# A two-block transformer forward pass: the query rotation later, the forget-gate sums in three pieces, one wide product per norm

## The chip, the cores and the metric

The kernel runs on one core of a Trainium2 chip. The metric is the device time of one execution in microseconds (us), the median of several runs. In the texts PE is TensorE, DVE is VectorE, ACT is ScalarE, POOL is GpSimd and SP is SyncE, which issues most of the transfers.

## The reference, cut to what matters

One sequence of 512 tokens and width 1024, all in float32, goes through two blocks. What the change touches is the root-mean-square norm ahead of each projection, the forget gate of the first attention and the rotation of the latent attention's queries:

```python
def rms_norm(x, g):
    y = x * lax.rsqrt(jnp.mean(x * x, axis=-1, keepdims=True) + NORM_EPS)
    return y * g

# first block, mixer
proj = xn @ w_in
qa, ka, va, fa, cq, ckv, kr, ga, gb = jnp.split(proj, splits, axis=-1)
log_f = jax.nn.log_sigmoid(fa + b_forget)
ya = forgetting_attention(qa, ka, va, log_f)      # uses c = cumsum(log_f) over the tokens
qb = rms_norm(cq, q_a_norm_g) @ w_q_up            # q_nope and q_rope of 8 heads
q_rope = apply_rope(q_rope, cos, sin)
kv = rms_norm(ckv, kv_a_norm_g) @ w_kv_up         # k_nope and v of 8 heads
yb = latent_attention(q_nope, q_rope, k_nope, rope(kr), v)
h = h + (gate_a * (ya @ w_branch_a) + gate_b * (yb @ w_branch_b)) @ w_out
h = h + swiglu(rms_norm(h, norm_ffn_g))
# second block: x + 0.5 swiglu(norm), a second mixer, x + 0.5 swiglu(norm), a last norm
```

## The kernel before, in words

The activations lie transposed, features on the 128 partitions and the 512 tokens on the free axis, as eight tiles of 128x512. To keep float32 accuracy at the speed of the reduced float32 type (F32R), every operand is split into a high and a low F32R part (ACT makes the high, DVE or POOL the low), and each product is three products (`mm3`): high by high, high by low, low by high. Weights stream from memory on SP's queue and are split by ACT (L235) and DVE (L236).

A planner places the instructions: the program is traced in order, and each engine's queue gets its instructions by that order, a later one being let ahead where the planner's own estimate says that an earlier one isn't ready. What is in a queue runs strictly in order. `weave` traces two generators in turn: the attention of 16 heads as the main one, and as filling the remaining projections (`pair`, `gates`, `prepare_b`).

The norm chain has four links. While the eight tiles of a hidden state come out of a projection, `sq_add` squares each on ACT (L449) and adds it to an accumulator on POOL (L451). `sum_rows` (L417) adds over the partitions with four one-column products against ones, in plain float32; the trace records each plain float32 product as two products. `rstd` makes the reciprocal root (L422 on DVE, the power on POOL, L411). `spread` turns the 128x4 result into a 128x512 tile with the same value on every partition: the values are split in two (L433 and L370), each part is multiplied into a diagonal (L437, tile `diag`), and two F32R products with ones (L440) add up the columns; ACT copies the sum out (L442). `spread` is called eight times: in `first_mixer`, twice in `prepare_b` (for the two latent norms), once in the first feed-forward stage, twice in the second, once in `second_mixer` and once in the last feed-forward stage. In the feed-forward stages it is a hook between two groups of 24 products.

`forget_rows` (called after the first of three latent groups, L828) makes the log forget gates, their running sums over the tokens with products against a triangle and ones (L1041, L1042), and turns them by transposes (L1057) into the tile `crow` (L1059). For each head a POOL transfer (L1089) brings two rows of `crow` into the keys' second tile, which the scores (L1095, L1096) read.

`prepare_b` makes the latent attention's inputs: both spreads, the query features (L852 evacuates on DVE), the rotated part `qr` (ACT, L867), `rope_q` (L868: four POOL and eight DVE operations, all of line L1003), the key features (L852 again), v (ACT, L876) and `rope_kr`, whose transposes are recorded at L692.

Of the kernel before, what the change touches and what calls it, by code (L numbers as in the profile page):

```python
# [333 lines left out]
class Build:  # L334
# [78 lines left out]
    def sum_rows(self, acc):  # L413

        b = self.bank("s")[:, 0:NT]
        for tt in range(NT):
            self.nc.tensor.matmul(b[:, tt:tt + 1], lhsT=acc[:, tt * P:(tt + 1) * P], rhs=self.ones[:, 0:1], start=True, stop=True)  # L417
        return b
# [8 lines left out]
    def spread(self, r, tag, pool=None):  # L427

        nc = self.nc
        b = self.bank("s")  # L430
        rh = self.small.tile([P, NT], F32R, tag="rh", name=self.nm("rh"), bufs=1)
        rl = self.small.tile([P, NT], F32, tag="rl", name=self.nm("rl"), bufs=1)
        nc.vector.tensor_copy(rh, r)  # L433
        self.lo(rl, r, rh)
        dg = self.small.tile([P, 2, 512], F32R, tag="diag", name=self.nm("diag"), bufs=1)
        for n, x in enumerate((rh.bitcast(F32), rl)):
            nc.vector.tensor_tensor(  # L437
                out=dg[:, n, :].rearrange("p (a b) -> p a b", a=NT), in0=self.ident[:, None, :].to_broadcast([P, NT, P]),
                in1=x[:, :, None].to_broadcast([P, NT, P]), op=ALU.mult)
            nc.tensor.matmul(b, lhsT=self.ones_r, rhs=dg[:, n, :], start=n == 0, stop=n == 1)  # L440
        o = (pool or self.small).tile([P, 512], F32, tag=tag, name=self.nm(tag), bufs=1)
        nc.scalar.copy(o, b)  # L442
        return o

    def sq_add(self, acc, x, first, scale=None, tmp=None, eng=None):

        nc = self.nc
        dst = acc if first else tmp if tmp is not None else self.small.tile([P, 512], F32, tag="sq", name=self.nm("sq"), bufs=1)
        nc.scalar.activation(dst, x, AF.Square, scale=1.0 if scale is None else scale)  # L449
        if not first:  # L450
            (eng or nc.gpsimd).tensor_tensor(out=acc, in0=acc, in1=dst, op=ALU.add)  # L451
# [269 lines left out]
    def load_start(self, yp):  # L721
# [42 lines left out]
        V.memset(self.halfpi, float(np.pi / 2))  # L764
        self.ones_r = one(P, "ones_r", F32R)
        return acc, xt
# [8 lines left out]
    def first_mixer(self, acc0, xt, ey, yp):  # L775
# [5 lines left out]
        for c in range(2):  # L781
            def ev(tt, b, c=c):
                if tt == 0 and c == 0:
                    self.r_tok = self.rstd(self.sum_rows(acc0), D)
                nc.scalar.activation(tokA[:, tt, c * 276:(c + 1) * 276], b, AF.Copy, scale=self.r_tok[:, tt:tt + 1])

            for _ in self.tokens(f"t1{c}", (2, 2, 2, 2) if c else self.FIRST, 276, self.xh, self.xl, self.TOKTAGS[c], ev):
                n += 1
                if n % 4 == 0 and self.squares:
                    self.squares.pop(0)()  # L790
            if c == 0:
                nc.gpsimd.tensor_copy(self.ones_r, self.ones)
                self.rb = self.spread(self.r_tok, "rb")
# [24 lines left out]
        for m in range(3):  # L818
# [8 lines left out]
            if m == 0:  # L827
                self.forget_rows(tokA, yp)  # L828

# [7 lines left out]
        def prepare_b():  # L837
# [21 lines left out]
            for t in range(2):  # L859
# [6 lines left out]
                for i in range(2):  # L866
                    nc.scalar.activation(qr[:, 2 * t + i, :], b[:, i * 256:(i + 1) * 256], AF.Copy, scale=rq[:, 2 * t + i:2 * t + i + 1])  # L867
            self.rope_q(qr)  # L868
            w = self.ws.next("kv")
            self.ws.run_ahead()  # L870
            yield from feats(1, w, ch[2:], cl[2:], rbkv)
            for tt in range(NT):
                b = self.bank("mm")
                sl = slice(tt * P, (tt + 1) * P)
                self.mm3(b, ch[2][:, sl], cl[2][:, sl], w[0][:, 0, 512:1024], w[1][:, 0, 512:1024], True, True)
                nc.scalar.activation(v[:, tt, :], b, AF.Copy, scale=rkv[:, tt:tt + 1])  # L876
                yield 640.0
            self.rope_kr(kr, yp)
            B["ready"] = True
# [147 lines left out]
    def forget_rows(self, tokA, yp):  # L1027
# [10 lines left out]
        V.tensor_scalar(out=f, in0=f, scalar1=0.0, scalar2=None, op0=ALU.min)  # L1038
        V.tensor_tensor(out=f, in0=f, in1=l, op=ALU.subtract)
        b = self.bank("s")  # L1040
        nc.tensor.matmul(b[:, 0:32], lhsT=self.cst[:, C_TRI:C_TRI + P], rhs=f, start=True, stop=True)  # L1041
# [10 lines left out]
        self.hi(cs[:, :, :, 0], c4, scale=-8.0)  # L1052
        self.lo(cs[:, :, :, 1], c4, cs[:, :, :, 0], scale=-8.0)
        b = self.bank("s")
        cs2 = cs.rearrange("p t h c -> p t (h c)").bitcast(F32)
# [104 lines left out]
    def out_product(self, key, mh, ml, src, gain, accs):  # L1160
# [5 lines left out]
        for m in range(KD):  # L1166
# [5 lines left out]
            self.put_x(m, xs[m], self.gain(gain, m))  # L1172
            self.sq_add(accs, xs[m], m == 0)

# [707 lines left out]
    def main(self):  # L1882
# [30 lines left out]
        def out0(m, x):  # L1913
            self.put_x(m, x, self.gg[:, m:m + 1])
            self.sq_add(acc1, x, m == 0)
            self.sq_add(acc2, x, m == 0, scale=gf(m))

        self.ffn("f0", 1.0, lambda m: self.gain("norm_ffn_g", m), [sums, spread], out0)
# [23 lines left out]
        def out1(m, x):  # L1942
            self.put_x(m, x, self.gain("mix_norm_2", m))
            self.sq_add(acc3, x, m == 0)
            nc.sync.dma_start(out=self.spill["x2"][m], in_=x)
# [120 lines left out]
```

## Time and profile before

| | us |
|---|---|
| median of 3 runs | 2049.75 |
| lowest and highest | 2049.63, 2051.26 |
| the profiled execution's own time | 2051.97 |
| its span, first to last instruction | 2050.2 |
| TensorE busy in the span | 2016.3 (98%) |
| VectorE, ScalarE, GpSimd busy | 1467.2, 1040.4, 549.4 |

The page gives busy time by engine first. The view of waits lists, for an engine, what ended its idle times. A timeline row has the start, the duration, the engine, the line, the operation with its output and inputs, the shape, the count and in brackets the idle time just before with what ended it. Products are pipelined: a 512-column product's record is 0.39 us long, but the next one starts about 0.23 us after it, so what a product costs is read from the start of the next. An idle time in brackets is therefore shorter by some 0.16 us than the slot that was lost.

### The profile page before, as it was taken

The page shows a single profiled execution, that of the slowest core. Times are in us where ns is not written, and L with a number is a line of the kernel's source. Part 1 is how long each engine was busy: PE and PEld are TensorE (multiplying, and loading weights), DVE is VectorE, ACT ScalarE, POOL GpSimd, SP SyncE. Part 2 cuts the span into 40 slices and gives each one's busy share as a digit, 9 for nine tenths or more (in the row PEclk, how much of TensorE's full clock was granted, in tenths as well). Part 3 has the DMA queues.
Part 4 walks back from the last instruction along what each step waited for, and adds up shares of the span by engine and source line. Part 5 has one row for each costly group of instructions (what it writes and reads, how often), then busy time and mean ns, then how long its engine had stood idle before and what let it go on. Part 6 is the DMA issues. An engine that isn't in the chain of part 4 may idle for free. (4 is left out here: it accounts for less than half of the span.)

```text
span 2050.2 us, 31305 instructions
## 1 busy us (share of the span) xinstructions
PE 2016.3 (98%) x11694; PEld 1743.6 (85%) x11694; DVE 1467.2 (72%) x2730; ACT 1040.4 (51%) x1944; POOL 549.4 (27%) x460
## 2 busy tenths in 40 slices
PE   9999999999999999999999999999999999999998
PEld 8787878899899889899987778888888888989997
DVE  7678776696587488568647799888557757856865
ACT  7666753354355436345434576666343333534554
POOL 2233233331232334023235211110312232412310
PEclk9999999999999999999999999999999999999999
DMA  7323254223233322433455322222543342233353
GB/s 205 75 68 97 88 159 139 83 81 110 93 104 117 118 70 90 116 100 106 121 169 145 96 58 82 78 67 72 171 133 104 118 154 72 91 107 99 104 176 125
DMA packets 229528, 223.60 MB, mean 109 GB/s; under 512 B 16785, under 2 KB 190993, under 8 KB 229377
## 3 DMA queue, kind: packets, MB, share of 16 engines
q1 hardware_dynamic: 222992, 203.94, 33.2%
q0 software_dynamic: 5024, 15.90, 2.4%
q8 instruction: 92, 1.51, 0.3%
q10 hardware_dynamic: 1360, 1.77, 0.3%
q14 instruction: 60, 0.48, 0.1%
HBM read 204.11 MB, written 14.68 MB: 107 GB/s over the span
## 5 line engine op out<-in xcount | busy, mean ns | idle before, releaser
L236 DVE TENSOR_TENSOR wl<-raw,wh 128x1024 fp32r<-128x1024 f32 (+5 forms) x267 | 320.2, 1201 | 166.9 <-ACT wh L235 164.7
L235 ACT CAST wh<-raw 128x1024 fp32r<-128x1024 f32 (+5 forms) x267 | 252.3, 948 | 359.9 <-PE mm L397 289.0
L396 PE MATMUL mm<-xh,wh 128*128 128x512 f32 x888 | 362.9, 409 | 1.8 <-ACT th L363 1.5
L397 PE MATMUL mm<-xl,wh 128*128 128x512 f32 x888 | 350.0, 395 | 1.9 <-DVE xl L370 1.9
L398 PE MATMUL mm<-xh,wl 128*128 128x512 f32 x888 | 350.2, 395 | 0.0
L303 POOL TENSOR_TENSOR wl<-raw,wh 128x512 fp32r<-128x512 f32 x102 | 133.6, 1331 | 279.3 <-PE mm L1195 145.7
L398 PEld LDWEIGHTS mm<-xh,wl 128*128 128x128 f32 x888 | 167.1, 188 | 35.5
L396 PEld LDWEIGHTS mm<-xh,wh 128*128 128x128 f32 x888 | 167.5, 189 | 30.1 <-ACT th L363 2.7
L397 PEld LDWEIGHTS mm<-xl,wh 128*128 128x128 f32 x888 | 167.8, 189 | 28.1 <-DVE xl L370 3.7
L397 PE MATMUL mm<-hl,wh 128*128 128x512 f32 x440 | 172.6, 392 | 0.8 <-DVE hl L372 0.8
L398 PE MATMUL mm<-hh,wl 128*128 128x512 f32 x440 | 172.7, 393 | 0.0
L396 PE MATMUL mm<-hh,wh 128*128 128x512 f32 x440 | 171.7, 390 | 0.0
L613 ACT ACTIVATE P<-s,st 128x128 f32<-128x128 f32 (+1 forms) x192 | 101.3, 529 | 59.0 <-DVE st L608 54.9
L303 POOL TENSOR_TENSOR wld<-raw,whd 128x512 fp32r<-128x512 f32 x51 | 71.6, 1404 | 220.2 <-DVE s13f L284 130.7
L1195 PE MATMUL mm<-th,wh 128*128 128x256 f32 x408 | 113.0, 277 | 0.0
L1195 PE MATMUL mm<-th,wl 128*128 128x256 f32 x408 | 112.8, 276 | 0.0
L1195 PE MATMUL pt<-xl,wh 128*128 128x256 f32 x408 | 112.8, 276 | 0.0
L1195 PE MATMUL pt<-xh,wl 128*128 128x256 f32 x408 | 112.8, 276 | 0.0
L1195 PE MATMUL mm<-tl,wh 128*128 128x256 f32 x408 | 112.8, 276 | 0.0
L1195 PE MATMUL pt<-xh,wh 128*128 128x256 f32 x408 | 112.8, 276 | 0.0
L363 ACT CAST ph<-pt 128x128 fp32r<-128x128 f32 x192 | 80.3, 424 | 54.0 <-PE pt L631 53.1
L451 POOL TENSOR_TENSOR sacc<-sacc,sq 128x512 f32<-128x512 f32 x36 | 57.4, 1593 | 165.6 <-ACT sq L449 162.9
(483 smaller groups left out, 5459.1 us busy)
## 6 DMA issues: line engine op xcount, KB each, us to landing
raw<-in_gu_f SPq DMA_DIRECT2D x132, 512.0 KB
raw<-in_w_in SPq DMA_DIRECT2D x79, 512.0 KB
raw<-in_ffn_w_down SPq DMA_DIRECT2D x22, 512.0 KB
raw<-in_ffn_w_down SPq DMA_DIRECT2D x24, 384.0 KB
sp_th<-gt SPq DMA_DIRECT2D x32, 256.0 KB
raw<-in_w_out SPq DMA_DIRECT2D x16, 512.0 KB
raw<-in_ffn_w_down SPq DMA_DIRECT2D x24, 320.0 KB
raw<-in_w_ffn_down SPq DMA_DIRECT2D x16, 384.0 KB
```

Source lines behind the costliest of these rows:

```text
L235: nc.scalar.copy(p[0][:, :nk * nc_], src)
L236: nc.vector.tensor_tensor(out=p[1][:, :nk * nc_], in0=src, in1=p[0][:, :nk * nc_].bitcast(F32), op=ALU.subtract)
L303: (eng or self.ws.b.nc.vector).tensor_tensor(out=p[1], in0=src, in1=p[0].bitcast(F32), op=ALU.subtract)
L363: self.nc.scalar.copy(out, in_)
L396: mm(acc, lhsT=lh, rhs=rh, start=start, stop=False)
L397: mm(acc, lhsT=lh, rhs=rl, start=False, stop=False)
L398: mm(acc, lhsT=ll, rhs=rh, start=False, stop=stop)
L451: (eng or nc.gpsimd).tensor_tensor(out=acc, in0=acc, in1=dst, op=ALU.add)
L613: nc.scalar.activation(p, b, AF.Exp, bias=st[:, 0:1], scale=-1.0, accum_out=st[:, 1:2])
L1195: self.nc.tensor.matmul(acc, lhsT=l[:, sl], rhs=r, start=start and k + n == 0, stop=k == 3 and n == 2, skip_group_check=True)
```

## The change

Three edits. `rope_q` moves from before the key features to after v. `forget_rows` becomes a generator with two stops, and each of the three latent groups is followed by its next piece. In the norm chain, `spread` makes one diagonal in plain float32 and one plain float32 product with ones in place of a split, two diagonals and two F32R products; the tile `ones_r` and its copy go. Where `leave` is set (the last of eight squares of four accumulators), the square isn't added by POOL: `sum_rows` takes it as a second operand and so has eight products where it had four. In the first feed-forward's output the two accumulators' squares change places.

```diff
     def sum_rows(self, acc):
         b = self.bank("s")[:, 0:NT]
+        parts = [acc] + ([self.left] if self.left is not None and self.left_of is acc else [])
         for tt in range(NT):
-            self.nc.tensor.matmul(b[:, tt:tt + 1], lhsT=acc[:, tt * P:(tt + 1) * P], rhs=self.ones[:, 0:1], start=True, stop=True)
+            for i, x in enumerate(parts):
+                self.nc.tensor.matmul(b[:, tt:tt + 1], lhsT=x[:, tt * P:(tt + 1) * P], rhs=self.ones[:, 0:1], start=i == 0, stop=i == len(parts) - 1)
         return b
...
     def spread(self, r, tag, pool=None):
         nc = self.nc
         b = self.bank("s")
-        rh = self.small.tile([P, NT], F32R, tag="rh", name=self.nm("rh"), bufs=1)
-        rl = self.small.tile([P, NT], F32, tag="rl", name=self.nm("rl"), bufs=1)
-        nc.vector.tensor_copy(rh, r)
-        self.lo(rl, r, rh)
-        dg = self.small.tile([P, 2, 512], F32R, tag="diag", name=self.nm("diag"), bufs=1)
-        for n, x in enumerate((rh.bitcast(F32), rl)):
-            nc.vector.tensor_tensor(
-                out=dg[:, n, :].rearrange("p (a b) -> p a b", a=NT), in0=self.ident[:, None, :].to_broadcast([P, NT, P]),
-                in1=x[:, :, None].to_broadcast([P, NT, P]), op=ALU.mult)
-            nc.tensor.matmul(b, lhsT=self.ones_r, rhs=dg[:, n, :], start=n == 0, stop=n == 1)
+        dg = self.small.tile([P, 512], F32, tag="diag", name=self.nm("diag"), bufs=1)
+        nc.vector.tensor_tensor(
+            out=dg.rearrange("p (a b) -> p a b", a=NT), in0=self.ident[:, None, :].to_broadcast([P, NT, P]),
+            in1=r[:, :, None].to_broadcast([P, NT, P]), op=ALU.mult)
+        nc.tensor.matmul(b, lhsT=self.ones, rhs=dg, start=True, stop=True)
...
-    def sq_add(self, acc, x, first, scale=None, tmp=None, eng=None):
+    def sq_add(self, acc, x, first, scale=None, tmp=None, eng=None, leave=False):
...
-        if not first:
+        if leave:
+            self.left, self.left_of = dst, acc
+        elif not first:
             (eng or nc.gpsimd).tensor_tensor(out=acc, in0=acc, in1=dst, op=ALU.add)
...
-        self.ones_r = one(P, "ones_r", F32R)
...
-                nc.gpsimd.tensor_copy(self.ones_r, self.ones)
...
             if m == 0:
-                self.forget_rows(tokA, yp)
+                forget = self.forget_rows(tokA, yp)
+            next(forget, None)
...
-            self.rope_q(qr)
             w = self.ws.next("kv")
             self.ws.run_ahead()
             yield from feats(1, w, ch[2:], cl[2:], rbkv)
...
                 yield 640.0
+            self.rope_q(qr)
             self.rope_kr(kr, yp)
...
         V.tensor_tensor(out=f, in0=f, in1=l, op=ALU.subtract)
+        yield
         b = self.bank("s")
         nc.tensor.matmul(b[:, 0:32], lhsT=self.cst[:, C_TRI:C_TRI + P], rhs=f, start=True, stop=True)
...
         self.lo(cs[:, :, :, 1], c4, cs[:, :, :, 0], scale=-8.0)
+        yield
         b = self.bank("s")
...
-            self.sq_add(accs, xs[m], m == 0)
+            self.sq_add(accs, xs[m], m == 0, leave=m == KD - 1)
...
             self.put_x(m, x, self.gg[:, m:m + 1])
-            self.sq_add(acc1, x, m == 0)
             self.sq_add(acc2, x, m == 0, scale=gf(m))
+            self.sq_add(acc1, x, m == 0, leave=m == KD - 1)
...
-            self.sq_add(acc3, x, m == 0)
+            self.sq_add(acc3, x, m == 0, leave=m == KD - 1)
```

## Rows read from the trace of the kernel before

**Rows 1.** The page's first part: busy time, share of the span, instructions.

```profile
PE 2016.3 (98%) x11694; PEld 1743.6 (85%) x11694; DVE 1467.2 (72%) x2730; ACT 1040.4 (51%) x1944; POOL 549.4 (27%) x460
```

**Rows 2.** What PE waited for: total us, times, longest; whole span.

```profile
PE mm L396 <- DVE feat L852: 3.4, 2, 2.7
...
PE mm L397 <- DVE xl L370: 1.9, 3, 1.4
...
PE s L1057 <- DVE fg_s L372: 1.5, 1, 1.5
...
PE s L1041 <- DVE fg L1039: 1.5, 1, 1.5
```

**Rows 3.** Timeline of PE, the sum in the first feed-forward stage.

```profile
379.48 0.95 PE L417 MATMUL pt<-cst,sacc 128*128 128x1 f32 x8
380.29 0.48 PE L396 MATMUL mm<-xh,wh 128*128 128x512 f32 x1
```

**Rows 4.** The same stage's spread on DVE and PE (two products recorded together).

```profile
382.06 0.69 DVE L437 TENSOR_TENSOR diag<-cst,rh 128x512 fp32r<-128x512 f32 x1
...
385.89 0.61 PE L440 MATMUL pt<-diag,ones_r 128*128 128x512 f32 x2
386.34 0.39 PE L396 MATMUL early<-xh,wh 128*128 128x512 f32 x1
```

**Rows 5.** Timeline of PE, the kernel's start: four plain float32 products, then F32R.

```profile
1.19 3.78 PE L730 MATMUL pt<-warm 128*128 128x256 f32 x8 [1.19 <-DVE first L732]
4.93 1.06 PE L584 MATMUL mm<-wh,xh 128*128 128x276 f32 x3
...
7.50 0.43 PE L585 MATMUL mm<-wl,xh 128*128 128x276 f32 x1
7.73 0.43 PE L586 MATMUL mm<-wh,xl 128*128 128x276 f32 x1
```

**Rows 6.** Timeline, the first mixer's renormed tiles.

```profile
38.99 0.50 PE L397 MATMUL mm<-xl,wh 128*128 128x512 f32 x1 [0.31 <-DVE xl L370]
```

**Rows 7.** Timeline, the forget gates' sums and the first head's scores.

```profile
54.63 0.41 PE L1041 MATMUL s<-fg,cst 128*128 128x32 f32 x2 [1.45 <-DVE fg L1039]
...
61.25 0.60 PE L1057 MATMUL s<-cst,fg_s 128*16 128x128 f32 x4 [1.54 <-DVE fg_s L372]
...
62.76 1.11 POOL L1089 DMA_DIRECT2D k<-crow  x2 [8.37 <-ACT crow L1059]
...
68.35 0.22 PE L1095 MATMUL s<-k,q 128*128 128x128 f32 x1
```

**Rows 8.** Timeline, the latent attention's rotation and what follows it.

```profile
159.07 2.35 DVE L1003 TENSOR_TENSOR qr<-qr,rt 128x256 f32<-128x256 f32 x2
...
162.07 0.50 PE L396 MATMUL mm<-wh,ch 128*128 128x512 f32 x1 [2.67 <-DVE feat L852]
...
164.61 0.63 PE L692 MATMUL pt<-cst,krs 128*64 128x128 f32 x4 [0.20 <-POOL krs L370]
...
173.56 0.60 PE L692 MATMUL pt<-cst,rs 128*64 128x128 f32 x4 [0.61 <-DVE pl L370]
```

**Rows 9.** Timeline, the second mixer: spread, renorm, the first compressed-key product.

```profile
1072.14 1.10 PE L440 MATMUL s<-diag,ones_r 128*128 128x512 f32 x2
...
1073.89 2.74 DVE L469 SCALAR_TENSOR_TENSOR xs<-xs,gains,rb 128x512 f32<-128x512 f32 x4
...
1098.76 0.36 PE L1625 MATMUL s<-w,blkhl 128*128 128x256 f32 x1 [2.37 <-DVE blkhl L370]
```

**Rows 10.** Stretches: us, PE busy (instructions), granted TensorE clock, DMA share, GB/s.

```profile
160.00:163.00 3.00, 0.93 (x4) 1.00 0.00 0
...
1098.70:1100.00 1.30, 1.24 (x7) 0.63 0.76 210
1100.00:1102.00 2.00, 2.00 (x9) 0.50 0.50 121
1102.00:1104.00 2.00, 2.00 (x10) 0.89 0.58 158
```

More of the change, by code (lines that the diff above doesn't have):

```diff
@@ L443, in spread @@
         return o
-    def sq_add(self, acc, x, first, scale=None, tmp=None, eng=None):
+    left = left_of = None
+    def sq_add(self, acc, x, first, scale=None, tmp=None, eng=None, leave=False):
         nc = self.nc
```

## The prediction

> **What bounds the kernel now.** I read the busy times first. TensorE is busy for 2016.3 of 2050.2 us [rows 1], so only 34 us of its idle time can be won at all, and every product that is added behind a TensorE that isn't waiting goes straight onto the end. The second view was TensorE's waits [rows 2]: the reader is to see which of them belong to lines of the diff. Two are the forget gates' products (L1041 and L1057, 1.45 and 1.54 us) and two the key features' evacuation, L852 (3.4 us together). None is for `sum_rows` (L417); the waits for `xl` (1.9 us, behind the renorm in both mixers) hang on `spread` only indirectly. The third view was the timeline around each of these places and around the eight spreads and the sums, which gives the prices. DVE (72%) and POOL (27%) bound nothing over the whole, so DVE and POOL operations that the norm chain loses are worth time only where TensorE waits for them.
>
> **The change, part by part.**
>
> *Last square by TensorE.* Four of the eight sums get four more products, each recorded twice. Eight such records took from 379.48 to 380.29, 0.81 us [rows 3], so this adds 0.81 us at four places, 3.2 us of TensorE. What it removes is one POOL addition in each; since no sum was waited for, that is worth nothing. Where TensorE has no wait behind it, the 0.81 us is paid in full.
>
> *Spread in one product.* It removes the split, one diagonal of 0.69 us on DVE and one F32R product. Before, the pair of products cost 0.45 us (385.89 to 386.34) [rows 4]. The new product is plain float32 with 512 columns, and the trace has none of that width at the full clock. The nearest row is the start of the kernel: eight records of 256 columns from 1.19 to 4.93, 0.47 us each, in a stretch where F32R products of 276 columns start 0.23 us apart, which is 1.2 GHz at a column per cycle [rows 5]. So a plain float32 record needs about two cycles per column, and 512 columns at 2.4 GHz again take 0.47 us; with two records the new product costs 0.94 us, 0.49 more than the pair. Eight times this is 3.9 us. The other end, a column per cycle, would make it equal to the pair, so the bounds are 0 and 3.9 us; I take 3.9, because the row is of the same kind of product.
>
> By place this gives:
> - First feed-forward: no wait anywhere near [rows 3, 4]. 0.81 + 0.49 = +1.3 us, and the same +1.3 us in the last one. The chain's shorter DVE part is hidden there either way: the first diagonal starts at 382.06 and the product stands in its place at 385.89, behind a group of 24 products [rows 4].
> - Second feed-forward: one longer sum and two spreads, 0.81 + 0.98 = +1.8 us. Together these three make +4.4 us.
> - `prepare_b`: two spreads, +1.0 us if nothing else moves, and 0 if the waits for the second diagonals that vanish make up for it. I take +0.5.
> - First mixer: +0.49 us, but TensorE waits for `xl` soon behind it (0.31 us named, 0.16 more hidden in the record) [rows 6], and the renorm isn't later. I take 0, between -0.3 and +0.5.
> - Second mixer: TensorE comes to the spread at 1072.14, waits there for the second diagonal (the pair's record is 1.10 us against 0.61 elsewhere [rows 4, 9]), and the renorm starts at 1073.89. With the longer sum TensorE comes 0.8 us later, at 1072.9; the product ends near 1074.0 instead of 1073.24, so the renorm starts 0.7 us later. Behind it TensorE waits for DVE (1.6 of the 1.9 us for `xl` [rows 2] and 2.37 us at 1098.76 [rows 9]), so the stage ends by DVE's chain: +0.7 us. The bounds are -0.9 (the diagonal and two small operations that DVE saves come out in full) and +1.3 (all of TensorE's extra work).
>
> The norm chain thus costs 4.4 + 0.5 + 0 + 0.7 = +5.6 us.
>
> *Forget gates in pieces.* Before, the products at L1041 and L1057 stand in TensorE's queue before their operands are there, and 24 products of the next latent group, some 5.5 us, stand behind them. Each piece now comes a group later. The two waits, 1.45 and 1.54 us [rows 7], go; I take -3.0. What is late next is `crow`: its transfer on POOL's queue was issued at 62.76 after POOL had waited 8.37 us, and the first scores read it at 68.35 [rows 7]. It will be some 4 us later, and POOL's next operations with it. The cover is the filling: TensorE has the next pair's 48 products to do in place of the scores. If the planner places the scores too early all the same, up to 3.0 us comes back; the bounds are -3.3 (with the hidden 0.16 each) and 0.
>
> *Query rotation later.* The two waits for L852 come from DVE doing the rotation (the last two operations alone took 2.35 us from 159.07) while three banks of key features wait to be evacuated [rows 8]. Behind the change the features go first, and 3.4 us, 3.7 with the hidden part, is free. What is late next: the rotated key's transposes (at 164.61, with 0.20 us of wait) stand behind the rotation on DVE and POOL, and the first use of the rotated queries stands at 173.56 [rows 8]. The latter has some 7 us to spare; the former has none, though gate products can be put ahead of it. I take -3.0, between -3.7 and +2.0.
>
> **The sum.** 5.6 - 3.0 - 3.0 = -0.4 us. On the profiled span of 2050.2 that is 2049.8, on its own time of 2051.97 it is 2051.6; the median of the runs stands 2.2 us below the profiled time, so I apply the difference to it: 2049.75 - 0.4 = 2049.4 us, no change that can be measured. A measurement of this kernel can tell about 0.2%, 4.1 us, from no change; that is 2045.6 on one side and 2053.9 on the other.
>
> **The rivals.**
>
> *The rotation only moves the wait* (slower). The eight DVE and four POOL operations still run, and the planner's estimate of them is too short, as the wait of 2.67 us shows [rows 8]. If TensorE meets the rotated key's transposes before its filling suffices, the wait is paid there, and up to 2.0 us more than before because features no longer lie between. It decides once the wait at L692 exceeds 5 us: 5.6 - 3.0 + 2.0 = +4.6, 2054.3 us. For it speaks that the transposes at 164.61 had no slack; against it, that only five gate products had been used as filling before them.
>
> *The order stays as it was.* The planner lets a later instruction ahead if it thinks it ready; if it puts the rotation and the sums where they were, only the costs remain: +5.6, 2055.3 us. Against it speaks that L1057 stands in the middle of a latent group that was traced after it, so the traced order counts.
>
> *DVE's lead in the second mixer comes out* (faster). If the spread isn't reached later than the diagonal, the stage gains 0.9 instead of losing 0.7, and with a shorter wait at 1098.76 the half-clock stretch behind it goes. Granted clock was 0.63, 0.50 and 0.89 over 1.3, 2.0 and 2.0 us there [rows 10], which cost 0.5 + 1.0 + 0.2 = 1.7 us. In all -0.4 - 1.6 - 1.7 = -3.7, 2046.0 us, at the border of what can be told.
>
> *The wide float32 product costs no more than the pair*: about 3.4 us of the 3.9 goes (the rest was covered), 2046.0 us.
>
> *A new half-clock stretch.* After 2.37 us of waiting at 1098.76 TensorE was granted 0.50 (1.2 of 2.4 GHz) for 1100 to 1102, yet in 160 to 163, with 0.93 us of work in 3 us, it kept 1.00 [rows 10]. Waits that move can therefore meet such a stretch or not; one more like the first costs 1.7 us: 2051.1 us. The Trainium skill ("TensorE: Matmul & The Clock Gate", Part 1: The HAM clock gate) says that the half rate is the array's default and sustained activity lifts it, so idle time is paid twice; by that rule a wait that is removed could be worth more than its length, and one that is made could cost more. The trace bears it out at 1098.76 and not at 162.07.
>
> **How the numbers follow.** Forecast 0.60; DVE's lead 0.13; the cheap product 0.06; the new stretch 0.07; the moved wait 0.08; the order unmoved 0.06. The second and third lie at the border of faster, so half of each counts there, with 0.06 from the forecast's own spread: 0.16 faster. The last two give 0.11 and the forecast 0.02: 0.13 slower. That leaves 0.71 for no change. The bounds of the unknown costs reach from 2045.2 (second mixer and the product at their good ends, in part) to 2053.6 (0.7 us more in three places and half of the moved wait); the range is that, and leaves out the two slow rivals and the far end of the fast ones, about 0.2.
>
> **What would show it.** After, the records of L440 should be eight pairs near 0.47 us from start to start, `sum_rows` in the feed-forward stages 1.6 us long instead of 0.8, the waits at L1041, L1057 and L852 gone, and a wait of under 1 us at L692. The feed-forward stages should each be 1.3 to 1.8 us longer and the first mixer 5 to 6 us shorter. I'm wrong if the first mixer gains much less, if wide products start 0.23 us apart, or if the second mixer's waits change by more than 1 us.

## The result, and the profile after

The changed kernel takes 2064.36 us (median, 2063.89 to 2066.09), the kernel before 2049.8: a ratio of 1.0066, 95% interval 1.0054 to 1.0078. The forecast was 2049.4 us with a range up to 2053.6, so it was wrong by some 15 us, and no rival came near. The profiled execution took 2063.89 us with a span of 2062.1, against 2051.97 and 2050.2 before: 11.9 us more between the two profiles, and 14.6 between the medians, since the profile of before stands 2.2 us above its median and that of after 0.5 us below.

The page's busy times of the changed kernel, to be laid beside [rows 1]:

```profile
PE 2031.1 (98%) x11726; PEld 1763.5 (86%) x11726; DVE 1462.8 (71%) x2706; ACT 1040.6 (50%) x1944; POOL 542.7 (26%) x455
```

TensorE is busy for 14.8 us longer with only 32 more records, which are the longer sums'. Its idle time didn't grow: 31 us against 34. So waits don't make up the loss; products got longer. The next reading is where. The stages are cut at the first record of each `sum_rows` but that of `prepare_b` (L417 before, L419 after):

| stretch, us | before | after | difference | forecast |
|---|---|---|---|---|
| start to the first sum | 21.67 | 21.41 | -0.3 | 0 |
| first mixer | 357.81 | 354.40 | -3.4 | -5.5 |
| first feed-forward stage | 342.11 | 348.17 | +6.1 | +1.3 |
| second feed-forward stage | 346.25 | 350.84 | +4.6 | +1.8 |
| second mixer | 634.02 | 633.29 | -0.7 | +0.7 |
| last feed-forward stage, to the end | 348.29 | 353.97 | +5.7 | +1.3 |

The three feed-forward stages have 11.9 us more than forecast between them. Inside them TensorE is hardly ever idle (0.6 us in the first one before), so the distances from each record's start to the next one's add up to the stage, and can be summed by kind:

| us in the stage | first: before, after | second: before, after | last: before, after |
|---|---|---|---|
| 1428 products of 256 columns (`quarter`) | 163.83, 170.51 | 165.02, 170.20 | 163.95, 170.52 |
| 512-column products, all kinds | 177.01, 175.50 | 172.83, 171.39 | 165.58, 163.62 |
| `sum_rows` | 0.81, 1.71 | 1.71, 2.60 | 0.81, 1.70 |
| `spread` | 0.45, 0.46 | 1.03, 1.02 | 0.47, 0.46 |

The norm chain is there as the diff has it: one longer sum in each stage, +0.9 us, and spreads that cost the same. What the diff doesn't touch at all moved by far more: `quarter`, the products of 128x256 of the feed-forward units (L1195 before, L1197 after), took 18.4 us longer over the three stages, and the 512-column ones 4.9 us less. The timeline of TensorE before (start, duration, line, output and inputs), at the end of one run and the start of the next:

```profile
443.04 0.28 PE L1195 MATMUL mm<-th,whd 128*128 128x256 f32 x1
443.16 0.28 PE L1195 MATMUL mm<-tl,whd 128*128 128x256 f32 x1
443.28 0.28 PE L1195 MATMUL mm<-th,wld 128*128 128x256 f32 x1
443.40 0.28 PE L1195 MATMUL mm<-th,whd 128*128 128x256 f32 x1
...
444.12 0.28 PE L1195 MATMUL mm<-th,wh 128*128 128x256 f32 x1
444.23 0.28 PE L1195 MATMUL mm<-tl,wh 128*128 128x256 f32 x1
444.34 0.28 PE L1195 MATMUL mm<-th,wl 128*128 128x256 f32 x1
444.46 0.28 PE L1195 MATMUL mm<-th,wh 128*128 128x256 f32 x1
444.57 0.28 PE L1195 MATMUL mm<-tl,wh 128*128 128x256 f32 x1
```

and after, products of the second kind:

```profile
441.35 0.28 PE L1197 MATMUL mm<-th,wh 128*128 128x256 f32 x1
441.46 0.28 PE L1197 MATMUL mm<-tl,wh 128*128 128x256 f32 x1
441.58 0.28 PE L1197 MATMUL mm<-th,wl 128*128 128x256 f32 x1
441.70 0.28 PE L1197 MATMUL mm<-th,wh 128*128 128x256 f32 x1
```

Before, products of `th` with `whd` start 0.120 us apart (0.36 for three) and those with `wh` 0.1133 (0.34 for three). After, those with `wh` take 0.12 as well, although the instructions are the same. This is where the time went. The difference is 6.7 ns a product, hard to see in a column in us, but the three stages have 4284 products of this line.

What could slow an untouched product? The diff removes tiles: `ones_r` (512 bytes of each partition), `rh` and `rl` (32 bytes each). In the compiled program everything that is allocated behind them lies lower: the weights' ring (`wh`, `wl`) by 512 bytes, the tiles of the stages by 576. Modulo 128 bytes that gives:

| start modulo 128 bytes | before | after |
|---|---|---|
| `xh`, `xl` | 0 | 0 |
| ring `wh`, `wl` | 64 | 64 |
| `th`, `tl`, `hh`, `hl`, `whd`, `wld` | 0 | 64 |

Before, `th` and `whd` start at the same place modulo 128 and their products were already slow; after, `th` and `wh` do too. So the theory to test: **a product is slower where its moving tile and its weights start at the same place modulo 128 bytes** (theory P). The rivals are the instructions that the change adds (N), and that the moving tile alone must start on a 128-byte line (M).

The rest of the profile after bears on the other two edits. TensorE's waits in the first mixer (22 to 385 us; total, times, longest), against [rows 2]:

```profile
PE pt L693 <- POOL krs L370: 2.5, 1, 2.5
PE mm L396 <- ACT gt L956: 1.8, 1, 1.8
PE s L1098 <- DMA k<-crow: 0.8, 1, 0.8
PE pt L632 <- DVE k L1017: 0.8, 1, 0.8
PE s L437 <- DVE diag L434: 0.7, 1, 0.7
PE mm L396 <- DVE feat L852: 0.6, 1, 0.6
```

The waits at the forget gates' products are gone, and the wait for `feat` went from 3.4 to 0.6 us. But 2.5 us now stand at the rotated key's transposes (`krs`, 0.2 before [rows 8]), and 0.8 us each at `crow`'s transfer and at the key tile. And the longer sum and the new spread (timeline):

```profile
375.81 0.28 PE L419 MATMUL pt<-cst,sacc 128*128 128x1 f32 x2
375.95 0.36 PE L419 MATMUL pt<-cst,sq 128*128 128x1 f32 x2
...
377.30 0.36 PE L419 MATMUL pt<-cst,sq 128*128 128x1 f32 x2
377.52 0.48 PE L396 MATMUL mm<-xh,wh 128*128 128x512 f32 x1
...
383.11 1.02 PE L437 MATMUL pt<-diag,cst 128*128 128x512 f32 x2
383.57 0.79 PE L396 MATMUL early<-xh,wh 128*128 128x512 f32 x1
```

The sum takes 1.71 us (0.81 in [rows 3]), as forecast. The wide plain float32 product takes 0.46 us from its start to the next product's, where the forecast had 0.94: it costs what the pair cost [rows 4].

### The profile page after: what moved, and what is told of

Its sections match the earlier page's. It is cut to its first block, busy times and chain, and to the rows that moved or that the text cites. A ratio compares the mean times of both kernels' runs of the same rounds, so it can differ in the third digit from the quotient of the medians.

```text
span 2062.1 us, 31349 instructions
## 1 busy us (share of the span) xinstructions
PE 2031.1 (98%) x11726; PEld 1763.5 (86%) x11726; DVE 1462.8 (71%) x2706; ACT 1040.6 (50%) x1944; POOL 542.7 (26%) x455
## 5 line engine op out<-in xcount | busy, mean ns | idle before, releaser
L1197 PE MATMUL mm<-th,wh 128*128 128x256 f32 x408 | 115.7, 284 | 0.0
L1197 PE MATMUL mm<-th,wl 128*128 128x256 f32 x408 | 115.7, 284 | 0.0
L1197 PE MATMUL mm<-tl,wh 128*128 128x256 f32 x408 | 115.4, 283 | 0.0
L1197 PE MATMUL pt<-xh,wh 128*128 128x256 f32 x408 | 114.4, 280 | 0.0
L1197 PE MATMUL pt<-xl,wh 128*128 128x256 f32 x408 | 113.8, 279 | 0.0
L1197 PE MATMUL pt<-xh,wl 128*128 128x256 f32 x408 | 113.8, 279 | 0.0
L609 DVE CUSTOM_DVE_ANT_0 s<-s,cst 128x128 f32<-128x128 f32 (+1 forms) x192 | 93.4, 489 | 12.1 <-PE s L1766 5.6
```

The costliest lines, as they stand in the source:

```text
L609: nc.vector.tensor_tensor_reduce(out=b, in0=b, in1=u["mask"][:, 512 - n:512], scale=-u["scale"], scalar=3.0e38, op0=ALU.add, op1=ALU.min, ...
L1197: self.nc.tensor.matmul(acc, lhsT=l[:, sl], rhs=r, start=start and k + n == 0, stop=k == 3 and n == 2, skip_group_check=True)
```

## The experiments

Each kernel was compared with the kernel before on the same chip. The pitch (start to next start) of its products is told as a mean in ns over the whole run; distances of 0.3 us or more are left out. A ratio is taken over all executions and not from two medians, so that the two can differ by 0.0004. In the table the places are those of the moving tile and the weights modulo 128.

| kernel | `th` with ring | `th` with `whd` | `xh` with ring | 512 columns, `hh` with ring | first feed-forward stage, us |
|---|---|---|---|---|---|
| before | 114.3 (0, 64) | 119.9 (0, 0) | 114.2 (0, 64) | 229.0 | 342.11 |
| after | 120.2 (64, 64) | 119.9 (64, 64) | 118.2 (0, 64) | 226.9 | 348.17 |
| after_pad64 | 114.3 (0, 64) | 119.9 (0, 0) | 114.4 (0, 64) | 228.9 | 343.06 |
| before_pad64 | 118.8 (64, 64) | 119.5 (64, 64) | 117.9 (0, 64) | 232.4 | 349.09 |
| before_pad64_all | 116.9 (64, 0) | 119.5 (64, 64) | 120.2 (0, 0) | 229.0 | 347.40 |
| before_pad32 | 119.9 (32, 64) | 119.7 (32, 32) | 118.1 (0, 64) | 233.3 | 350.42 |
| norm_only | 114.1 (0, 64) | 119.9 (0, 0) | 114.1 (0, 64) | 229.0 | 342.70 |
| d_other_half | 113.8 (0, 64) | 113.8 (0, 64) | 113.9 (0, 64) | 229.5 | 340.88 |
| after_places | 114.0 (0, 64) | 114.0 (0, 64) | 114.0 (0, 64) | 229.5 | 342.18 |

One column doesn't follow from the places of a product's own two tiles. In the changed kernel `xh` went from 114.2 to 118.2 ns with its places as they were, 7.3 us on 1836 products; those of `th` give 10.8 us. Both go back in after_pad64, which moves the feed-forward tiles and not `xh`. So products at equal places are slow themselves, and where they are many, those that run among them are slower too.

### The changed kernel with its tiles put back

```diff
         V.memset(self.halfpi, float(np.pi / 2))
+        V.memset(self.small.tile([P, 16], F32, tag="pad", name="pad", bufs=1), 0.0)
```

> The changed kernel with one more 64-byte tile, unused but for a memset, in the pool that lies ahead of the feed-forward stage's tiles, so that these start 64 bytes later, at the places modulo 128 bytes that they had before. Theory P (places): the change frees 576 bytes ahead of them, and a 256-column product of the feed-forward stages takes 120.0 ns instead of 113.3 or 117.8 where its moving tile and its weights start in the same half of a 128-byte line. By it the three stages' 4284 quarter products go back from a mean of 119.3 to 115.0 ns (-18.5 us) and some 1300 products of 512 columns from 226.9 to 229.0 ns (+2.7 us): 15.8 us less than the changed kernel, 2048.6 us, a ratio to the kernel before of 0.999. Rival N (instructions): the 14.5 us come from what the change adds to the norm chain, then 64 bytes change nothing: 2064.4 us, a ratio of 1.007. Rival M (the moving tile alone must start on a 128-byte line): as P here.

Measured: 2051.64 us against 2051.96, a ratio of 1.0002 (0.9993 to 1.0011), where the changed kernel had 1.0066. One unused tile of 64 bytes takes away all of the loss that can be measured. The groups of `quarter` from 440 to 660 us (count, then duration in ns: lowest, median, highest; first and last start), of the changed kernel:

```profile
L1197 PE MATMUL mm<-th,wh x128: 277/283/290, 441.3 to 656.8; 128*128 128x256 f32 x128
L1197 PE MATMUL pt<-xh,wh x128: 280/280/283, 442.8 to 655.3; 128*128 128x256 f32 x128
L1197 PE MATMUL mm<-th,whd x64: 278/283/283, 439.9 to 651.1; 128*128 128x256 f32 x64
```

and with the pad:

```profile
L1198 PE MATMUL mm<-th,wh x128: 276/276/279, 443.9 to 653.7; 128*128 128x256 f32 x128
L1198 PE MATMUL pt<-xh,wh x128: 276/276/279, 445.3 to 652.4; 128*128 128x256 f32 x128
L1198 PE MATMUL mm<-th,whd x68: 278/283/287, 442.4 to 659.3; 128*128 128x256 f32 x68
```

The durations say what the pitch says: 276 is the fast kind, 279 to 280 the middle one, 283 the slow one. Only `whd` stays slow. N has fallen.

### The kernel before with its tiles moved

```diff
         V.memset(self.halfpi, float(np.pi / 2))
+        V.memset(self.small.tile([P, 16], F32, tag="pad", name="pad", bufs=1), 0.0)
```

> The kernel before with the same unused 64-byte tile, and nothing else: the feed-forward tiles move into the same half of a 128-byte line as the weights. Theory P: the quarter products of the three stages go to 120 ns and 118 ns as in the changed kernel, +18.5 us, the 512-column products behind them to 226.9 ns, -2.7 us: 2065.5 us, a ratio of 1.0077. Rival M: the same. Rival N: 2049.8 us, 1.000.

Measured: 2072.81 us against 2051.96, 1.0101 (1.0084 to 1.0118), and 21.3 us more between the two spans (2071.5 against 2050.2). So nothing but the places is needed, and they cost even more here than in the changed kernel. The groups of `quarter` from 440 to 660 us:

```profile
L1196 PE MATMUL mm<-th,wh x128: 279/280/287, 440.8 to 658.0; 128*128 128x256 f32 x128
L1196 PE MATMUL mm<-tl,wh x128: 274/282/285, 440.9 to 658.1; 128*128 128x256 f32 x128
```

The sizes missed the expectation both ways: `quarter` takes 14.9 us more over the three stages instead of 18.5, the 512-column products there 3.7 us more instead of 2.7 less, and the first mixer, where no change was expected, is 2.0 us longer. The products of `hh` take 232.4 ns where the changed kernel has 226.9. The places of these two kernels are the same modulo 128 only: in the compiled programs `th` and `hh` lie 0 from the ring's weights modulo 256 in the changed kernel and 128 in this one. Modulo 128 alone therefore doesn't settle the pitch, and whether the distance modulo 256 does wasn't tried by itself.

### Ring and tiles moved together

```diff
         V.memset(self.halfpi, float(np.pi / 2))
+        V.memset(one(16, "pad"), 0.0)
```

> The kernel before with an unused 64-byte tile further ahead, behind the tiles xh and xl, so that the weights' ring and the feed-forward tiles move by 64 bytes together and only xh and xl stay. Theory P: th and hh against the weights stay as they were (113.3 or 117.8 ns, 512 columns 229 ns); the quarter products of xh and xl (1836) go from 114.2 to 120 ns, +10.7 us, and the 512-column products of xh and xl (some 2570 in the mixers and elsewhere) from 231 to 227 ns, -10 us: about 2050.5 us, a ratio of 1.000, with the products of xh at 120.0 ns and those of th at 113.3. Rival M: xh keeps its line, th and hh leave theirs: products of th at 120 ns, 2058 to 2065 us. Rival N: 2049.8 us and no product's pitch changed.

Measured: 2063.60 us, 1.0056 (1.0041 to 1.0071). Groups as above:

```profile
L1196 PE MATMUL mm<-th,wh x130: 276/280/283, 439.9 to 660.0; 128*128 128x256 f32 x130
...
L1196 PE MATMUL pt<-xh,wh x128: 277/283/290, 447.0 to 659.2; 128*128 128x256 f32 x128
```

The slow kind went over to `xh`, which didn't move at all: its weights came to its place. `th`, which left its 128-byte line, isn't at 120 but at 116.9. So it is the distance of the two starts that counts, and not the place of the moving tile alone. By the time alone M would have stood: 2063.60 us lies in its 2058 to 2065 and 13 us off P's 2050.5. It has fallen by the pitches, since by M `xh` stays fast and `th` takes 120 ns. P's total was mis-sized twice: `th` runs in part at the middle pitch (2.6 ns more, 1836 products, 4.8 us), and the 512-column products of `xh` gained 1 ns (231.0 to 230.0) and not 4.

### Is it the half of the line?

```diff
+        V.memset(self.small.tile([P, 8], F32, tag="pad", name="pad", bufs=1), 0.0)
```

> The kernel before with an unused tile of 32 bytes instead of 64, so that th, hh, whd and wld start at 32 modulo 128 and the weights' ring stays at 64. If only the half of the line counts in which a tile starts: th against the ring as before (113.3 or 117.8 ns), with whd and wld 120 ns, 2050 us. If it is the distance of the two starts, 32 bytes being too near: th against the ring at 120 ns or between, 2055 to 2070 us.

A single execution: 2078.31 us, a span of 2076.5, the slowest of all; it is read for its pitches. Starts 32 bytes apart (32 and 64) are no better than equal ones for 256 columns (119.9 ns) and worse for 512 (up to 237.4 ns for `hl` with `wh`, 233.3 over the three kinds). "The same half of a 128-byte line", as the expectations put theory P, is thus too narrow: of the distances tried, 64 bytes is good, 0 and 32 are bad.

### The norm chain alone

The change's `sum_rows`, `sq_add` and `spread`, with `ones_r` and a pad for `rh` and `rl` kept; forget gates and rotation as before. Against the changed kernel:

```diff
+        self.ones_r = one(P, "ones_r", F32R)
...
+        V.memset(self.small.tile([P, 16], F32, tag="pad", name="pad", bufs=1), 0.0)
...
-            next(forget, None)
...
+            self.rope_q(qr)
             w = self.ws.next("kv")
```

> The norm chain's part of the change alone (last square by TensorE, one plain float32 product per spread), with the freed tiles' places kept by unused tiles so that every other tile lies where it lay before; forget gates and rotation as before. The prediction's sum: +5.6 us, 2055.4 us, a ratio of 1.0027. Rival N: most of the 14.5 us and the 6 us that the other two parts gain, +15 to +20 us, 2065 to 2070 us. If the wide products or the longer sums are covered by waits that go: +2 us or less.

Measured: 2053.31 us, 1.0010 (1.0001 to 1.0020), +2.1 us with bounds of 0.2 and 4.1 (1.4 by the medians); the spans differ by 1.0. The forecast for this part was +5.6. The sums cost 0.89 us more in each of four places, as said; the eight wide products take 0.455 to 0.54 us each, so that their +3.9 us isn't there (start of the product to start of the next, 0.45 us):

```profile
385.94 1.02 PE L437 MATMUL pt<-diag,cst 128*128 128x512 f32 x2
386.39 0.80 PE L396 MATMUL early<-xh,wh 128*128 128x512 f32 x1
```

### The forget gates alone

```diff
-                self.forget_rows(tokA, yp)
+                forget = self.forget_rows(tokA, yp)
+            next(forget, None)
...
+        yield
         b = self.bank("s")
```

> The kernel before with the forget gates' sums in three pieces and nothing else; no tile moves. The prediction: both waits (L1041, L1057) go and the scores have filling ahead of them, -3.0 us, 2046.8 us, a ratio of 0.9985, and the first mixer (from the first sum at L417 to that of the first feed-forward stage) 354.8 us long where it was 357.8. Rival (part comes back): the changed kernel waits 0.8 us for the transfer of crow's rows ahead of a score and 0.8 us for the key tile, so that -1.4 us remain, 2048.3 us, 0.9993, the first mixer 356.4 us.

Measured: 2048.57 us against 2050.93, 0.9986 (0.9977 to 0.9996). The waits from 50 to 80 us, where the kernel before had the two of 1.5 us [rows 2]:

```profile
PE s L1099 <- DMA k<-crow: 0.8, 1, 0.8
PE s L1060 <- DVE fg_s L372: 0.2, 1, 0.2
```

Of 3.0 us, 1.0 came back at once, as the rival had it: from the first sum to `prepare_b`'s the stretch is 2.1 us shorter (117.69 to 115.58). From there to the feed-forward stage it is 1.1 us longer; where, wasn't found. The first mixer has 356.78 us (the rival's 356.4), 1.0 less than before, and the ratio, whose interval holds both, is nearer to the forecast's only because other stages, which the edit doesn't reach, came out 0.2 to 0.7 us shorter each. That much must be taken as the scatter of a stage between two kernels.

### The rotation alone, and in another place

```diff
-            self.rope_q(qr)
             w = self.ws.next("kv")
...
+            self.rope_q(qr)
             self.rope_kr(kr, yp)
```

> The kernel before with the query rotation behind v and nothing else; no tile moves. The prediction: the two waits for the key features' evacuation go, -3.0 us, 2046.8 us, 0.9985. Rival (the wait moves): TensorE waits some 2.5 us for the rotated key's transposes instead of 0.2 and 0.6 us for the features instead of 3.4, -0.5 us or less, 2049.3 us, 0.9998, the first mixer 357.3 us.

Measured: 2048.84 us, 0.9990 (0.9981 to 0.9999), an interval that holds both forecasts; the spans differ by 1.3 us and the first mixers by 0.6 (357.81 to 357.18). The waits in the first mixer:

```profile
PE pt L692 <- POOL krs L370: 2.8, 1, 2.8
PE mm L396 <- ACT gt L956: 2.2, 1, 2.2
...
PE pt L631 <- DVE k L1017: 1.3, 1, 1.3
```

and the first of them in the timeline:

```profile
165.78 0.63 PE L692 MATMUL pt<-cst,krs 128*64 128x128 f32 x4 [2.75 <-POOL krs L370]
```

TensorE no longer waits for the features, but 2.8 us for `krs` and 1.3 for the next head's key tile (`k`): the rival. Twelve products of `xh` and `xl` with `wh` and `wl`, gate products, stand between v's products and these transposes, with four scores and six products of probabilities and values, where the kernel before had three gate products alone; the wait came all the same. Two more kernels on top of `d_other_half` (below) asked whether another order would do. With the edit's own order:

> d_other_half with the query rotation where the change puts it (behind v, ahead of the rotated key). The wait only moves: -0.3 to -1 us against d_other_half, a ratio of 0.996 to 0.9965, with 2.4 to 2.8 us of wait at the key's transposes. By the prediction's -3.0 us: 0.995.

Measured: 2044.07 us against 2050.47, 0.9971 (0.9959 to 0.9984), against 0.9965 without the rotation moved, which the intervals don't tell apart; the wait at the key's transposes is 2.4 us and the first mixer 0.7 us shorter (355.94 to 355.24), as expected. With the rotation behind the rotated key:

```diff
-            self.rope_q(qr)
             w = self.ws.next("kv")
...
             self.rope_kr(kr, yp)
+            self.rope_q(qr)
```

> d_other_half (forget gates in pieces, one wide product per spread, sums as before, whd and wld 64 bytes further) with the query rotation moved behind the rotated key, thus behind v and the key's transposes. Theory for the rotation: the wait that the change takes from the key features (3.4 us to 0.6) comes back at the key's transposes (2.5 us) only because the key's rotation stands behind the queries' on DVE and POOL; with the two the other way round both waits are short, -2.5 to -3 us against d_other_half, a ratio of 0.995. Rival: the first use of the rotated queries, 9 us behind the key's transposes in the kernel before, now waits instead: no gain, 0.9965.

Measured: 2042.53 us, 0.9962 (0.9949 to 0.9975), again not told apart from 0.9965, and a first mixer of 356.99 us against 355.94. The waits:

```profile
PE mm L399 <- ACT gt L954: 2.7, 1, 2.7
PE s L1095 <- POOL rt L1001: 1.8, 1, 1.8
```

The waits for `feat` and `krs` are gone, and a score waits 1.8 us for the queue of POOL, which is still at the rotation (`rt`). Put in any of the three places, the rotation's work on DVE and POOL makes TensorE wait for something.

### The slow products that the kernel before had already

If places decide, `whd` and `wld` can be moved too. The base of this kernel has the forget gates in pieces, the one-product spread, the sums as before, and a pad that keeps the other places.

```diff
+        V.memset(self.small.tile([P, 16], F32, tag="pad", name="pad", bufs=1), 0.0)
...
-        h, lo = (pool.tile([P, 512 if ring else 1024], F32R, ...
+        h, lo = (pool.tile([P, 528 if ring else 1024], F32R, ...
+        if ring:
+            o = 16
+            h, lo = h[:, o:o + 512], lo[:, 16 - o:528 - o]
```

> A kernel with the forget gates in pieces, one wide product per spread, the sums as before, and all places of before modulo 128 bytes, but the weights whd and wld of the feed-forward units, which start 64 bytes further, so that they no longer begin in the half of a 128-byte line in which th and tl begin. Theory P, simplest form (each product by its own two places): the 612 products with whd and wld go from 120 to 113.3 ns, -4.1 us, with the forget gates and the wide product 2043 to 2045 us, a ratio of 0.997. Rival S (a state that lasts): in the kernel before the quarter products run at 117.8 ns at a stage's start and at 113.3 ns only behind one or two runs of products at 120.0; if these runs are what brings the faster pitch, all 4284 products stay at 117.8 ns, +10.5 us on the mean of 115.3, 2058 us, 1.004.

Measured: 2044.10 us against 2050.93, 0.9965 (0.9952 to 0.9978), 6.8 us faster than the kernel before, of which `quarter` has 5.1 in the trace (492.8 to 487.7 us over the three stages). Groups as above:

```profile
L1195 PE MATMUL mm<-th,wh x128: 276/276/276, 442.2 to 650.7; 128*128 128x256 f32 x128
...
L1195 PE MATMUL mm<-th,whd x68: 276/276/281, 440.8 to 656.2; 128*128 128x256 f32 x68
```

All kinds of `quarter` are fast, and the three stages have a mean of 113.8 ns where the kernel before had 115.0. Rival S, that runs of products at 120.0 ns are needed to bring the fast pitch, has fallen: the stages start at 117.8 ns, go over to 113.3 without such products and stay there but for the first products of each stage and a few at its end. A variant kept the slow places for the first three units of each stage (`o = 0 if i % 17 < 3 else 16`):

> The same kernel, but in the first three units of each feed-forward stage whd and wld begin in the same half as th, as before, and in the other fourteen in the other half. Theory P, simplest form: as d_other_half but with 108 products at 120 ns: 2044 to 2046 us. Rival S (a state that lasts): behind the runs at 120.0 ns in the first three units the products go to 113.3 ns and stay there: 2044 to 2046 us too, and then this kernel is some 12 us faster than d_other_half; if the state is lost again in some unit, the products behind it run at 117.8 ns to the stage's end.

Measured: 2047.95 us, 0.9987 (0.9978 to 0.9996), slower than either forecast of 2044 to 2046 us. In the first stage its products ran at 117.8 ns through these units and several behind them (972 of 1428 at 113.3, against 1308). In the kernel before, where such runs at 120.0 ns come in all units, 1128 are at 113.3. So the runs at 120.0 ns aren't needed for the fast pitch, and they alone don't decide which of the two comes behind them.

The whole change with all of these places:

> The changed kernel, all of it, with the feed-forward tiles at their places of before modulo 128 bytes and whd and wld 64 bytes further, as in d_other_half. Theory P: 612 products of whd and wld at 113.3 instead of 120 ns and fewer at 117.8, so 4 to 6 us less than after_pad64, a ratio of 0.998 to 0.9975 to the kernel before, which is the change's own worth once no product pays for its place. If the gain of d_other_half came from elsewhere: 1.000.

Measured: 2050.89 us against 2050.47, 1.0003 (0.9993 to 1.0012). P's time was missed: the ratio is that of the other branch, no better than after_pad64's 1.0002 on another chip. The pitches are as P has them: `quarter` is at 114.0 ns, 488.4 us over the three stages where after_pad64 has 493.2, and the span is 2.6 us shorter; where the rest of the 4 to 6 us went is open. Against `d_other_half` this kernel still has the last squares on TensorE and the rotation moved. The three feed-forward stages and the second mixer are 1.30, 1.26, 1.30 and 1.42 us longer than there (342.18 against 340.88 in the first): 5.3 us. The sums' records account for 0.89 in each. The rest isn't in one place: in the first feed-forward stage it stands in the 512-column products of `hh` and `hl` (121.62 against 121.17), in the other two in `quarter` (0.37 and 0.29 us), so it can't be put down to the sums.

## Why the prediction was wrong

**The failed step** is the sum itself. It is built from the instructions that the diff adds, removes and moves, and takes it for granted that every other instruction keeps the duration it had: "no wait anywhere near", "0.81 + 0.49 = +1.3 us". That `ones_r`, `rh` and `rl` go was known; what they were counted for is the operations that go with them, not the room that they leave. That 576 bytes fewer ahead of the stages' tiles bring `th` to the place of the ring's weights modulo 128 was the larger part of the change: 18.4 us on `quarter`, less 4.9 on the 512-column products. The trace of before had the clue, two pitches of 0.113 and 0.120 us for products of one shape, within one line, with no wait; the prediction didn't read that line, because the diff doesn't touch it. After_pad64 and before_pad64 show it from both sides, one with the change and without the loss, the other the reverse. Why equal places cost time inside the chip stays open.

With the places kept, the change is worth +0.4 us (1.0002, bounds -1.4 and +2.3; -0.3 by the medians), and the forecast was -0.4. That agreement is luck and isn't to be taken for the steps being right; several were off and cancelled:

- *Spread in one product.* Mis-sized: 0.94 us each from [rows 5], 0.455 measured. Of +3.9 us nothing is left: the condition of the rival "costs no more than the pair", given 0.06, came true. The row was of the same kind of product, but of the kernel's start, where a record of 256 columns takes 0.43 us on the way; here two records of 512 columns together take 0.456. The prediction halved for the clock, and another factor of two remains that no run here explains. The profile's granted clock for that stretch is 1.00, so that the reading as 1.2 GHz rested on the spacing of the F32R products alone. The Trainium skill ("FP8 and Floating Point Precision", TensorE Precision Notes) gives true float32 four passes through the array; by that an estimate for 512 columns at 2.4 GHz would be 0.85 us, and the measurement of 0.456 in two records decides against it here.
- *Last square by TensorE.* 0.81 forecast, 0.89 measured in the records, 3.6 us for the four. The 5.3 us between after_places and d_other_half aren't the sums' price: norm_only, which has the same sums, is only 2.1 us (0.2 to 4.1) longer than the kernel before. It is the one part that gave TensorE more to do, and no sum had been waited for.
- *Forget gates.* -3.0 forecast, the bound of 0 named; -1.0 measured in the first mixer. The two waits went but for 0.2 us, and 0.8 us at `crow`'s transfer came in their place, the transfer that the prediction had named as late next, so the filling covered it only in part. Another 1.1 us came back behind `prepare_b`, and where isn't known.
- *Rotation.* -3.0 forecast, -0.6 measured in the first mixer. Here the rival's mechanism was the right one: the wait moved to the transposes at L692 (2.5 to 2.8 us instead of 0.2). It was short of the 5 us at which the rival would have cost more than it saved. The prediction saw that these transposes had no slack and counted on gate products that could be put ahead of them. Twelve were, instead of three, and didn't suffice.
- *Second mixer.* +0.7 forecast, -0.7 measured, and -1.1 in norm_only; the scatter of a stage is as large as that, so neither sign is shown. DVE's lead didn't come out as a whole: the wait at the second of the two places is 2.4 us, as in [rows 9].

So two of the prediction's signs of being wrong came too. One was "if the first mixer gains much less": it gained 3.4 us instead of 5 to 6, and 2.0 in after_pad64. The other was "if wide products start 0.23 us apart": the two records of one take 0.456 us together. Either alone would have moved the time by some 2 to 4 us, inside the range.

## What to carry to other kernels

A change that adds or drops a tile moves every tile allocated behind it, and products that it doesn't touch became slower or faster by up to 6% each here. Look at the starts of the moving tile and the weights modulo 128 in both programs before summing instructions, and where a small edit costs much, put the places back with an unused tile and time that first. In the same way, two pitches for one shape within one line of a trace are a gain that lies open: moving two tiles by 64 bytes took 6.1 ns from each of 612 products here, which the times of d_other_half show and those of after_places don't.

## What the runs showed of the hardware

- Products of 128x256 on F32R tiles, back to back, ran mostly at three pitches: 113.3, 117.8 and 120.0 ns. Where moving tile and weights start at the same place modulo 128 bytes, the mean is 118.8 to 120.2 (the lowest in before_pad64, where they are 128 apart modulo 256 and single products take 115 to 122); 32 bytes apart, 119.9; 64 bytes apart, 113.3 or 117.8. The last two alternate without any change of places and last for hundreds of products, with 113.3 the rule where no product is at 120.0 (1308 of 1428 in the first stage of d_other_half) and 117.8 between many products at 120.0 (after: `xh` at 118.2, its places unchanged). What switches them wasn't found.
- Products of 512 columns of `hh` and `hl` have 226.9 ns (after) or 232.4 (before_pad64) at equal places modulo 128, 229 at 64 bytes, 233.3 at 32; those of `xh` and `xl` 231.0 at 64 and 230.0 at equal places. Equal places modulo 128 gave two pitches, so something else has a part in it, perhaps the distance modulo 256. Modulo 128 no other distances than 0, 32 and 64 were tried.
- The Trainium skill ("TensorE: Matmul & The Clock Gate", Part 2: What happens when you issue a matmul) says that loading the next weights takes no read bandwidth in SBUF from the running product. The runs put a doubt beside that: all that before_pad64_all changed in the places of `xh` and `wh` was that of the weights, and the pitch went from 114.2 to 120.2 ns. That it is the two reads that collide is argued, not shown.
- A plain float32 product of 512 columns takes 0.455 to 0.46 us in two records where nothing is waited for, no more than two F32R products (0.45 to 0.47).
